# Expert layers: where the modulation's shift is added to the gathered tokens

## Chip, cores and metric

One core of a Trainium2 chip runs the whole program, in one launch. The metric is the device time of an execution in microseconds (us); the time before is the median of three runs.

## What is computed

Two blocks of two layers each work on 512 tokens of 1024 features. The change concerns the first block, whose two layers each end in a mixture of 16 experts. Every token goes to two experts, after a norm and a modulation: a scale and a shift per feature, the same for all tokens.

```python
h = modulate(rms_norm(x, norm_ffn_g[i]), sh2, sc2)      # h * (1 + scale) + shift
x = x + g2[:, None, :] * hier_moe(h, moe_wg[i], moe_bg[i], moe_we[i], moe_be[i],
                                  moe_w_gate[i], moe_w_up[i], moe_w_down[i])
...
for e in range(N_EXPERTS):
    a = jax.nn.silu(t @ w_gate[e]) * (t @ w_up[e])
    out = out + combine[:, e:e + 1] * (a @ w_down[e])
```

## The kernel before

The kernel is written in a tile framework: a scheduler puts the instructions of each engine in a fixed order when the program is built, and assigns the tiles of a pool to its buffers then. Each engine runs its own list in that order and waits on semaphores.

An expert layer (`moe`, layers 0 and 1) computes only the tokens that an expert was given. The norm's scaled tokens, without the shift, are written to DRAM (`h2d`). For each expert GpSimd (POOL) issues a `gather` (L969): an indirect DMA that brings the expert's 128 rows of tokens into a tile `xg`, 128 tokens by 1024 features, 512 KB. `moe_xt` then turns `xg` feature-major: eight transposes of 128x128 on TensorE (PE) in two halves `xT` (`moe_xt1`, L1120). In each half a matmul follows that multiplies `shT`, the shift as rows on 16 partitions, with `shs`, a selection of these rows, and so adds the shift to the transposed tokens in PSUM (L206, `xT<-shs,shT`). ScalarE (ACT) and VectorE (DVE) split the half into a high part `xh` (ACT, L221) and a low part `xl` (DVE, L222); float32 products are made of three matmuls of such parts (`mm3`).

Layer 0 has 17 blocks of this kind (16 experts and a spare block for an expert that holds over 128 tokens), layer 1 has 16: 33 in all. I call each a round. A round's weights come in six chunks of 512 KB: four of gate and up (`gu`), two of down (`dn`). SyncE (SP) loads them into a ring of buffers: five `raw` tiles, two `xt` tiles, and `NRING` tiles (7 before) of the pool "pair", which has 25 tiles of 128x1024 and also holds `xg`, `xh`, `xl` and the results `Y`. Each chunk is split by ACT (`wh<-pre`) and DVE (`wl<-pre,wh`) into one of four pairs of `wsplit` tiles, which PE frees as it goes. On PE a round is: the transposes of the next round's tokens, 12 `gu` matmuls, two transposes `aT` of the round before, 12 more `gu` matmuls, 12 `dn` matmuls of the round before. ACT also evacuates `Y<-dn` and takes the Silu (`sg`); POOL issues the store of each `Y` to DRAM (L1166).

Before the rounds of a layer the router's results are turned into lists of tokens (`route`, `slots`), and `overflow` places a branch that is taken only when an expert holds more than the blocks there are. All engines read a number (`eid`) that DVE wrote and pass that branch. `GA = 4` gathers are asked for ahead of the rounds.

Of the kernel before, what the change touches and what calls it, by code (L numbers as in the profile page):

```python
# [9 lines left out]
FT = mybir.dt.float32  # L10
# [31 lines left out]
class First:  # L42
    """The first products W^T x after a norm, from x as it is: the factor per token comes after the products. The first
    four tiles of columns are fed tile by tile of x, as they become final."""

    def __init__(self, k, W, cols, scale, shift=None):
        """shift: a shift after the norm and a bias of the products; what both add to the products is left in bias."""
        self.k, self.W, self.cols, self.scale, self.shift = k, W, cols, scale, shift
        self.in_moe = False
        self.R, self.P, self.w, self.bias, self.S, self.n = [], {}, [], None, None, 0  # L50

    def feed(self, k, h=None):
        """Tile k of x is final, or half h of its tokens."""
        K = self.k
        n, hs = (512, 0) if h is None else (256, h)
        per = 512 // n
        cs = slice(hs * n, hs * n + n)
        if k == 0:
            self.P[hs] = [K.acc("f") for _ in range(4 // per)]
        if k % 4 == 0 and not hs:  # L60
            for ci, c in enumerate(self.cols):
                self.w.append(K.wtiles(self.W, D, k, 4, c, use=lambda r, k0: self.shifted(r, k0, ci, 2),
                                       q=K.nc.gpsimd if k and WL & 1 and self.in_moe else None)[0][1])
        if not hs:
            self.R.append(K.p("xr"))
        a = self.R[k]
        ah, al = a[:, cs], a[:, 512 + cs.start:512 + cs.stop]
        K.split(K.x[k][:, cs], ah, al, self.scale(k))
        for i in range(4):
            o = k % 4 * 256 + i % 2 * 128  # L70
            wh, wl = (y[:, o:o + 128] for y in self.w[k // 4 * 2 + i // 2])
            K.mm3(self.tile(i, hs, n), wh, wl, ah, al, k == 0 and i % per == 0,
                  k == KD - 1 and i % per == per - 1)
        if k == KD - 1 and cs.stop == 512:
            self.biases(4)
            self.w = None

    def shifted(self, raw, k0, ci, n):
        """The shift times four tiles by 256 columns, a quarter of the partitions each."""
# [27 lines left out]
    def tiles(self, rB):  # L107
        """Yields the four products, scaled, in SBUF."""
# [9 lines left out]
    def more(self, cols, rB):  # L118
        """Yields four more."""
# [16 lines left out]
class Base:  # L136
# [29 lines left out]
    def filter_done(self):  # L166
        """The filter's banks go to the products and the rest."""
        self.fctx.close()
        self.xp = self.pool("extra", 2)
        self.banks(self.ctx, acc=AC, misc=8 - AC)  # L170
# [46 lines left out]
    def split(self, src, h, l, scale=None):  # L217
        """src (times a per-partition scale) = h + l, both of 12 significant bits."""
# [13 lines left out]
    def wload(self, dma, n=1024, alloc=None, use=None):  # L232
        """Load n columns per partition and split them."""
# [18 lines left out]
    def wtiles(self, W, K, k0, kt, c0, alloc=None, use=None, q=None):  # L252
        """Chunks of at most 4 k-tiles by 256 columns."""
# [8 lines left out]
    def fm(self, W, c0, ncols, acts, k0=0, kt=8, K=1024):  # L262
        """Feature-major products: yields (tile, PSUM) per 128 columns of W."""
# [13 lines left out]
    def fm2(self, W, c0, ncols, acts, k0=0, kt=8, K=1024, pools=()):  # L277
        """As fm, all columns with half the tokens before the other half: yields (tile, half, PSUM)."""
# [32 lines left out]
    def rstd_from(self, ss, n):  # L311
        """ss: the sums of squares of eight tiles, or tiles whose sum over tiles and partitions is it, per token."""
# [22 lines left out]
    def norm_sb(self, ss, n):  # L335
        """The factor per token: on partitions, and as a row on all partitions."""
# [7 lines left out]
    def norm_half(self, ss, n, h, r, R=None, more=()):  # L344
        """The same for half h of the tokens; the row stays in PSUM unless R is given."""
# [18 lines left out]
    def sq_acc(self, ss, src, h=None):  # L364
        """Square a tile, or half h of its tokens; four at a time are summed over the partitions."""
# [12 lines left out]
    def flow(self, tasks, window):  # L378
        """Tasks (generators) started in order, one a round, at most window of them at a time, a stage a round each."""
# [26 lines left out]
    def range_red(self, w, k):  # L406
        """w modulo 2 pi, in [-pi, pi]."""
# [30 lines left out]
class Mla:  # L438
# [7 lines left out]
    def ada_vec(self, i, nm):  # L446
        """A modulation vector of layer i: 256 of its values in each quarter of the partitions."""
# [58 lines left out]
    def x_in(self):  # L506
        """The input, feature-major, split, and the first norm's factor per token."""
# [53 lines left out]
    def rope_apply(self, out, y, nm, t, nh, u=None):  # L561
        """Rotate y (heads of 64) into both halves of out (heads of 2 x 64)."""
# [12 lines left out]
    def mla_pre(self, r1, H, out):  # L575
        """Latents, and the keys, values and queries of two heads."""
# [98 lines left out]
    def kv(self, g, c, out, done):  # L675
        """Keys and values of two heads, as tasks."""
# [42 lines left out]
    def queries(self, g, cT, out, done):  # L719
        """Queries of two heads, as tasks."""  # L720
# [49 lines left out]
    def attend(self, KP, o, K, V, Q, QP):  # L770
        """Two heads, as tasks of a head and 128 queries."""
# [53 lines left out]
    def resid(self, W, acts, i, g):  # L825
        """x += g * (W^T acts); the squares' sums for the next norm."""
# [26 lines left out]
NRING = 7  # L853
# [3 lines left out]
class Moe:  # L857
# [3 lines left out]
    def moe_consts(self):  # L861
# [12 lines left out]
        self.shT = [None, None]  # L874
        self.shs = self.const("shs", [16, 8], FR)
        nc.vector.tensor_add(self.shs, self.ident[:16, 0:8], self.ident[:16, 8:16])
# [12 lines left out]
    def router_prep(self, i):  # L889
        """Fold the modulation into the router: scaled weights, and the bias of the shift."""  # L890
# [8 lines left out]
    def router(self):  # L899
        """Router products with tokens on the partitions."""  # L900
# [8 lines left out]
    def moe_pre(self, i):  # L909
        """Before the products that end in x: the shift as a row, the first weights."""  # L910
        nc = self.nc
        sh = self.mod[i][:, ADA_OFF["sh2"]:ADA_OFF["sh2"] + 8]
        w = self.sm("sh", 16)
        self.split(sh, w[:, :8].bitcast(FR), w[:, 8:].bitcast(FR))
        P = self.ps("shT")
        nc.tensor.transpose(P[:16, :128], w, self.ident)
        self.shT[i] = self.const(f"shT{i}", [16, 128], FR)
        nc.scalar.activation(self.shT[i], P[:16, :128], AF.Copy)
# [7 lines left out]

    def moe_x(self, i, k):
        """As each tile of x is final: scale it, and multiply with the router."""
# [17 lines left out]
    def moe_load(self, i, ec, kind):  # L946
        """Load a chunk into a tile of one of three pools."""
# [5 lines left out]
    def chunk_dma(self, raw, i, e, c, q=None):  # L953
        """Two k-tiles of gate and up (c < 4), or a k-tile of down."""
# [4 lines left out]
    def moe(self, i, ss, first=None):  # L959
# [7 lines left out]
        def gather(e):  # L967
            xg[e] = self.p("xg", FT)
            nc.gpsimd.indirect_dma_start(out=xg[e], out_offset=None, in_=self.h2d[i],  # L969
                                         in_offset=bass.IndirectOffsetOnAxis(ap=idx[e], axis=0))  # L970

# [41 lines left out]
        for t in range(NT):  # L1013
# [10 lines left out]
            nc.scalar.dma_start(self.h2d[i][t * 128:(t + 1) * 128, :], ht)  # L1024
        self.slots(R, 0, 2, idx)
# [6 lines left out]
        for e in range(2, GA):  # L1032
            gather(e)
        XT[0] = self.moe_xt(xg.pop(0))
        prev = None
        for e in range(N):
# [4 lines left out]
            if e + GA < N and e + GA > 1:  # L1041
                gather(e + GA)
            at = []
# [16 lines left out]
        if N > 16:  # L1060
            w = [self.wload(lambda r, c=c: self.chunk_dma(r, i, self.edyn, 4 + c, nc.scalar)) for c in range(2)]
        C = self.combine_load(i, R)
# [8 lines left out]
    def moe_zero(self):  # L1071
        """The row of a product that comes in another way."""
# [44 lines left out]
    def moe_xt1(self, X, a, P):  # L1117
        """Half of a block's tokens' features, feature-major, with the shift."""
        for k in range(4):
            self.nc.tensor.matmul(P[:, k * 128:(k + 1) * 128], X[:, (a * 4 + k) * 128:(a * 4 + k + 1) * 128], self.ident,  # L1120
                                  is_transpose=True, start=k == 0, stop=False)
        self.mm(P, self.shT[self.li][:16, :], self.shs[:16, a * 4:a * 4 + 4][:, :, None].to_broadcast([16, 4, 128]),
                False, True)
# [144 lines left out]
    def pieces(self, src, dst):  # L1268
        """Three bfloat16 pieces whose sum is src."""
# [46 lines left out]
    def overflow(self, i, R, spare):  # L1316
        """Blocks of 128 tokens of the experts that hold more than 128, under a branch. With a spare block
        the first of them is among the experts, and always computed (its slots may all be empty)."""
# [69 lines left out]
        def block(j):  # L1388
# [4 lines left out]
                                         in_offset=bass.IndirectOffsetOnAxis(ap=q[16], axis=0))  # L1393
            for a, P in enumerate((P0, P1)):
# [33 lines left out]
        def finish(idx, late):  # L1428
            """The spare block's slots, and the row of each product of each token."""
# [34 lines left out]
    def combine(self, i, C, L, first):  # L1464
        """The sum of each token's products into x; with products to come, half the tokens before the other."""
# [62 lines left out]
class Hyena:  # L1528
# [13 lines left out]
    def filter_gen(self, z, w, tn, nd):  # L1542
# [21 lines left out]
        def taps(o, c2, i):  # L1564
            """Filter responses of a channel tile, split into even and odd taps, position-major."""
# [189 lines left out]
    def table(self, src, split, whole):  # L1755
        """A table and its two parts."""
# [88 lines left out]
class Mix:  # L1845
# [13 lines left out]
    def first(self, kind, l):  # L1859
        """The first products after a norm in layer l."""  # L1860
# [9 lines left out]
    def tail(self, z, zs, prod, evac, g, nxt):  # L1870
        """The last columns of z, x += rmsnorm(z) * g and the next norm's factor, half the tokens after the other."""
# [38 lines left out]
    def conv(self, y, src, taps, bias=None):  # L1910
        """Causal: y[t] = sum_d taps[d] src[t-d], the first tap on ScalarE."""
# [269 lines left out]
def blocks(W):  # L2181
    """[K, N] as contiguous blocks of 256 columns by up to 4 x 128 rows, a row of the block per partition."""
# [9 lines left out]
def layout(I):  # L2192
    """The inputs as the kernel loads them: moved, padded with zeros and repeated, never computed with."""
# [125 lines left out]
```

## Time and profile before

| | |
|---|---|
| three runs | 2946.20, 2946.41, 2952.02 us; median 2946.41 |
| profiled execution | its span, first to last instruction, 2939.1 us; what lies around the span is 7.3 us against the median |
| PE busy | 2806.4 us (95%) |
| DVE busy | 1914.6 us (65%) |
| ACT busy | 1300.5 us (44%) |
| POOL busy | 144.8 us (5%) |
| rounds' transposes, layer 0 | first at 448.7 us, last at 614.8 us of the span |
| rounds' transposes, layer 1 | first at 1011.95 us, last at 1166.3 us of the span |

No separate time is given for the profiled execution, so its own time is taken as the span, and the median of the runs as the time to which differences are added. "Busy" counts the time in which an engine has at least one instruction under way. Averages over the whole span hide the stage at hand: in the rounds DVE is far busier than 65%.

### The profile page before, as it was taken

The page shows a single profiled execution, that of the slowest core. Times are in us where ns is not written, and L with a number is a line of the kernel's source. Part 1 is how long each engine was busy: PE and PEld are TensorE (multiplying, and loading weights), DVE is VectorE, ACT ScalarE, POOL GpSimd, SP SyncE. Part 2 cuts the span into 40 slices and gives each one's busy share as a digit, 9 for nine tenths or more (in the row PEclk, how much of TensorE's full clock was granted, in tenths as well). Part 3 has the DMA queues.
Part 4 walks back from the last instruction along what each step waited for, and adds up shares of the span by engine and source line. Part 5 has one row for each costly group of instructions (what it writes and reads, how often), then busy time and mean ns, then how long its engine had stood idle before and what let it go on. Part 6 is the DMA issues. An engine that isn't in the chain of part 4 may idle for free.

```text
span 2939.1 us, 38010 instructions
## 1 busy us (share of the span) xinstructions
PE 2806.4 (95%) x14430; PEld 2223.5 (76%) x14430; DVE 1914.6 (65%) x3260; ACT 1300.5 (44%) x2222; POOL 144.8 (5%) x191
## 2 busy tenths in 40 slices
PE   6899988999999799899999999999999999999998
PEld 2666766767866577678887888888878888888887
DVE  5776748986776498579935486264679645484363
ACT  4566746874312488443224354243343224353341
POOL 0111001110000111200000000000000000000000
PEclk8999998999999899999999999999999999999999
DMA  6666368962443498422222223223222332132321
GB/s 209 220 216 218 113 232 283 388 257 76 160 157 127 146 356 338 151 94 79 100 92 89 83 74 108 93 90 97 80 83 83 101 100 86 58 103 93 106 90 47
DMA packets 128148, 416.96 MB, mean 142 GB/s; under 512 B 13888, under 2 KB 24336, under 8 KB 127952
## 3 DMA queue, kind: packets, MB, share of 16 engines
q1 hardware_dynamic: 96128, 335.06, 32.9%
q0 software_dynamic: 12304, 44.58, 4.1%
q10 hardware_dynamic: 19520, 34.76, 3.4%
q8 instruction: 117, 1.92, 0.3%
q14 instruction: 79, 0.65, 0.1%
HBM read 380.78 MB, written 33.56 MB: 141 GB/s over the span
## 4 chain that ended last, share of the span: by engine, by line
PE 61%; DVE 2%; POOL 1%; issue 1%; DMA 0%; ACT 0%; POOLq 0%; DVEq 0%
PE acc L206 46%; PE gu L206 3%; PE f L206 3%; PE v L206 2%; PE dn L206 1%; PE ss L206 1%; PE nh L206 1%; PE xT L1120 1%; PE o L206 1%; DVE pre L1855 0%; PE S L206 0%; PE xT L206 0%; DVE uy L1918 0%; DMA y<-ys,pos 0%; PE bc L206 0%
## 5 line engine op out<-in xcount | busy, mean ns | idle before, releaser
L206 PE MATMUL acc<-X,wh 128*128 128x512 f32 x2432 | 755.8, 391 | 0.8 <-ACT X L221 0.7
L222 DVE TENSOR_TENSOR wl<-raw,wh 128x1024 fp32r<-128x1024 f32 (+1 forms) x338 | 411.2, 1220 | 408.2 <-ACT wh L221 396.6
L221 ACT ACTIVATE wh<-raw 128x1024 fp32r<-128x1024 f32 (+2 forms) x362 | 370.2, 1027 | 449.5 <-PE acc L206 376.0
L206 PEld LDWEIGHTS acc<-X,wh 128*128 128x128 f32 x2432 | 454.8, 188 | 97.6 <-issue 2.2
L206 PE MATMUL acc<-X,wl 128*128 128x512 f32 x1216 | 473.9, 390 | 0.0
L206 PEld LDWEIGHTS acc<-X,wl 128*128 128x128 f32 x1216 | 228.4, 188 | 47.1
L222 DVE TENSOR_TENSOR wl<-pre,wh 128x1024 fp32r<-128x1024 f32 x184 | 222.0, 1223 | 31.0 <-ACT wh L221 27.2
L206 PE MATMUL acc<-f,wh 128*128 128x512 f32 (+1 forms) x912 | 228.7, 349 | 0.0
L221 ACT ACTIVATE wh<-pre 128x1024 fp32r<-128x1024 f32 x184 | 191.4, 1058 | 37.3 <-PE gu L206 33.2
L206 PEld LDWEIGHTS acc<-f,wh 128*128 128x128 f32 x912 | 157.0, 189 | 25.2 <-issue 3.3
L2086 DVE SCALAR_TENSOR_TENSOR cfa<-sb,par,cfa 128x511 f32<-128x511 f32 (+15 forms) x240 | 163.2, 733 | 1.8 <-ACT cfa L2081 1.8
L206 PE MATMUL acc<-xr,wh 128*128 128x512 f32 x448 | 138.9, 391 | 0.0
L206 PE MATMUL acc<-f,wl 128*128 128x512 f32 (+1 forms) x384 | 136.4, 355 | 0.0
L1918 DVE SCALAR_TENSOR_TENSOR uy<-acc,par,uy 128x511 f32<-128x511 f32 (+1 forms) x128 | 95.7, 748 | 58.5 <-ACT uy L1914 56.3
L206 PE MATMUL f<-xr,wh 128*128 128x256 f32 x640 | 126.7, 291 | 1.8 <-ACT xr L224 1.8
L206 PE MATMUL gu<-wh,xh 128*128 128x512 f32 x264 | 112.1, 425 | 1.9 <-ACT wh L221 1.9
L206 PEld LDWEIGHTS f<-xr,wh 128*128 128x128 f32 x640 | 102.1, 192 | 13.5 <-issue 9.1
L206 PE MATMUL gu<-wl,xh 128*128 128x512 f32 x264 | 106.3, 403 | 0.9 <-DVE wl L222 0.8
L206 PE MATMUL gu<-wh,xl 128*128 128x512 f32 x264 | 106.6, 404 | 0.0
L206 PEld LDWEIGHTS acc<-xr,wh 128*128 128x128 f32 x448 | 83.9, 188 | 18.4 <-issue 1.2
L206 PE MATMUL f<-xr,wl 128*128 128x256 f32 x320 | 91.1, 286 | 0.0
L206 PE MATMUL acc<-xr,wl 128*128 128x512 f32 x224 | 87.6, 391 | 2.4 <-DVE wl L222 2.4
(511 smaller groups left out, 5153.9 us busy)
## 6 DMA issues: line engine op xcount, KB each, us to landing
pre<-in_moe SPq DMA_DIRECT2D x184, 512.0 KB, 8.1
raw<-in_w_in SPq DMA_DIRECT2D x106, 512.0 KB, 3.3
raw<-in_ada_w SPq DMA_DIRECT2D x96, 512.0 KB, 5.0
raw<-in_w_up SPq DMA_DIRECT2D x88, 512.0 KB, 3.3
raw<-in_w_down SPq DMA_DIRECT2D x40, 512.0 KB, 3.4
ys<-Y POOLq DMA_DIRECT2D x28, 512.0 KB, 7.1
raw<-in_hy_w_in SPq DMA_DIRECT2D x22, 512.0 KB, 3.6
kd<-K ACTq DMA_DIRECT2D x32, 256.0 KB, 2.5
```

The costliest lines, as they stand in the source:

```text
L206: return self.nc.tensor.matmul(o, a, b, start=st, stop=sp)
L221: nc.scalar.activation(h, src, AF.Copy)
L222: nc.vector.tensor_sub(l, src, h.bitcast(FT))
L1120: self.nc.tensor.matmul(P[:, k * 128:(k + 1) * 128], X[:, (a * 4 + k) * 128:(a * 4 + k + 1) * 128], self.ident, is_transpose=True, start=k ...
L1918: nc.vector.scalar_tensor_tensor(y[:, d:], src[:, :512 - d], taps[d], y[:, d:], op0=OP.mult, op1=OP.add)
L2086: v.scalar_tensor_tensor(c[j][:, d:], glu[i][:, :512 - d], self.pc(f"cf_conv_w{l}", (30 - d) * 4 + i), c[j][:, d:], op0=OP.mult, op1=OP.add)
```

## The change

The tokens get their shift in SBUF, right after they were gathered, and the matmul into the transposes goes. `shift_row` spreads the shift as one row over all 128 partitions (`shB`, a tile of the pool "pair", made by eight matmuls of 128x128 and two copies by ACT). `shift(e)` adds it to `xg[e]`: one TENSOR_TENSOR of 128x1024 in float32, on DVE for the first round of a layer, on POOL for all others. `NRING` goes from 7 to 6. `shT`, `shs` and their preparation in `moe_pre` go. Docstrings were taken out as well, which moves line numbers: the gather keeps L969, the add is L973, the transposes become L215, the store of `Y` L1171.

```diff
-NRING = 7
+NRING = 6
...
     def moe_pre(self, i):
-        nc = self.nc
-        sh = self.mod[i][:, ADA_OFF["sh2"]:ADA_OFF["sh2"] + 8]
-        w = self.sm("sh", 16)
-        self.split(sh, w[:, :8].bitcast(FR), w[:, 8:].bitcast(FR))
-        P = self.ps("shT")
-        nc.tensor.transpose(P[:16, :128], w, self.ident)
-        self.shT[i] = self.const(f"shT{i}", [16, 128], FR)
-        nc.scalar.activation(self.shT[i], P[:16, :128], AF.Copy)
...
+    def shift_row(self, i):
+        self.shB = self.p("shB", FT)
+        for a in range(2):
+            P = self.ps("shB")
+            for k in range(4):
+                self.mm(P[:, k * 128:(k + 1) * 128], self.m_(i, "sh2", a * 4 + k).to_broadcast([128, 128]), self.ident,
+                        True, True)
+            self.nc.scalar.activation(self.shB[:, a * 512:(a + 1) * 512], P, AF.Copy)
...
+        def shift(e, eng=nc.gpsimd):
+            eng.tensor_tensor(xg[e], xg[e], self.shB, op=OP.add)
...
+        self.shift_row(i)
         self.slots(R, 0, 2, idx)
...
         for e in range(2, GA):
             gather(e)
+        for e in range(GA - 1):
+            shift(e, nc.gpsimd if e else nc.vector)
         XT[0] = self.moe_xt(xg.pop(0))
...
             if e + GA < N and e + GA > 1:
                 gather(e + GA)
+            if e + GA <= N:
+                shift(e + GA - 1)
...
+        self.shB = None
         C = self.combine_load(i, R)
...
     def moe_xt1(self, X, a, P):
-        for k in range(4):
-            self.nc.tensor.matmul(P[:, k * 128:(k + 1) * 128], X[:, (a * 4 + k) * 128:(a * 4 + k + 1) * 128], self.ident,
-                                  is_transpose=True, start=k == 0, stop=False)
-        self.mm(P, self.shT[self.li][:16, :], self.shs[:16, a * 4:a * 4 + 4][:, :, None].to_broadcast([16, 4, 128]),
-                False, True)
+        self.tr4(P, [X[:, (a * 4 + k) * 128:(a * 4 + k + 1) * 128] for k in range(4)])
```

Two places show how the instructions move.

POOL in the middle of layer 0, before: `xg` tiles are gathered, `Y` tiles are stored, and nothing waits for a gather on this engine.

```order
L969 DMA xg1304_6289<-h2d0_360,ix1243_6070 128x1024
L1166 DMA ys0_362<-Y1301_6271 128x1024
L969 DMA xg1334_6397<-h2d0_360,ix1243_6070 128x1024
L1166 DMA ys0_362<-Y1331_6379 128x1024
L969 DMA xg1377_6648<-h2d0_360,ix1370_6539 128x1024
L1166 DMA ys0_362<-Y1361_6487 128x1024
```

The same place in the change:

```order
L969 DMA xg1274_6173<-h2d0_358,ix1243_6063 128x1024
L1171 DMA ys0_360<-Y1271_6155 128x1024
L973 TENSOR_TENSOR xg1274_6173<-xg1274_6173,shB1095_4893 128x1024
L969 DMA xg1304_6280<-h2d0_358,ix1243_6063 128x1024
L1171 DMA ys0_360<-Y1301_6262 128x1024
L973 TENSOR_TENSOR xg1304_6280<-xg1304_6280,shB1095_4893 128x1024
```

Each add stands behind the gather of the very tile that it works on, and ahead of the next gather, so POOL waits there for the transfer to land.

DVE ahead of the branch of layer 0, before: the lists of rounds 2 and 3 (`oh`) are partly made ahead of the branch (`eid` is the number that it reads, `ovx` the places of the combine).

```order
L1282 TENSOR_TENSOR oh1136_5652<-iotab_341,rb1082_4839 128x512
L1272 CAST rw1084_4845<-M1079_4816 128x64
L1330 CAST eid1105_4943<-ovf1104_4938 128x1
L1434 SCALAR_TENSOR_TENSOR ovx1106_4959<-iotas_337,M1079_4816 128x64
L1437 TENSOR_TENSOR ovx1106_4959<-M1079_4816,ovx1106_4959 128x64
L1438 TENSOR_REDUCE ovx1106_4959<-ovx1106_4959 128x4
L1331 TENSOR_LOAD eid1105_4943
L1421 COMPARE_AND_BRANCH
```

And in the change:

```order
L1444 TENSOR_REDUCE ovx1107_4963<-ovx1107_4963 128x4
L1445 TENSOR_SCALAR ovx1107_4963<-ovx1107_4963 128x8
L1446 SCALAR_TENSOR_TENSOR ovx1107_4963<-ovx1107_4963 128x8
L973 TENSOR_TENSOR xg1103_4923<-xg1103_4923,shB1095_4893 128x1024
L1336 TENSOR_LOAD eid1106_4947
L1427 COMPARE_AND_BRANCH
```

The first round's add stands ahead of the branch on DVE and waits for that round's gather; the four `oh` that stood there stand behind the branch now.

## Rows read from the trace of the kernel before

**Rows 1.** Windows: busy us and count of each engine, clock, DMA share, GB/s
```profile
core 0: us, PE busy (x) PEld busy (x) DVE busy (x) ACT busy (x) POOL busy (x), PEclk, DMA share, GB/s
560.00:600.00 40.00, 40.00 (x184) 30.82 (x183) 35.91 (x41) 33.68 (x47) 4.23 (x6) 1.00 1.03 418
1120.00:1160.00 40.00, 40.00 (x185) 30.94 (x185) 35.98 (x39) 33.41 (x47) 3.20 (x5) 1.00 1.03 419
```

**Rows 2.** Timeline of PE, one round: start us, duration us, engine, line, op
```profile
573.38 0.50 PE L206 MATMUL gu<-wh,xh 128*128 128x512 f32 x1
...
576.40 0.48 PE L206 MATMUL gu<-wh,xh 128*128 128x512 f32 x1
...
582.49 0.48 PE L206 MATMUL xT<-shs,shT 16*128 16x512 f32 x1
582.90 0.66 PE L1120 MATMUL xT<-par,xg 128*128 128x128 f32 x4
583.49 0.48 PE L206 MATMUL xT<-shs,shT 16*128 16x512 f32 x1
583.89 0.50 PE L206 MATMUL gu<-wh,xh 128*128 128x512 f32 x1
```

**Rows 3.** Timelines of ACT and DVE in the same round
```profile
573.98 2.00 ACT L221 ACTIVATE wh<-pre 128x1024 fp32r<-128x1024 f32 x2
...
575.07 3.50 DVE L222 TENSOR_TENSOR wl<-pre,wh 128x1024 fp32r<-128x1024 f32 x3 [0.26 <-ACT wh L221]
```

**Rows 4.** Groups by shape on DVE: count, busy us, mean ns, idle before
```profile
L222 DVE TENSOR_TENSOR wl<-pre,wh 128x1024 fp32r<-128x1024 f32 x184 | 222.0, 1223 | 31.0 <-ACT wh L221 27.2 <-DMA pre<-in_moe 0.4
L222 DVE TENSOR_TENSOR xl<-xT,xh 128x512 fp32r<-128x512 f32 x66 | 43.1, 684 | 5.0 <-ACT xh L221 4.4
...
L222 DVE TENSOR_TENSOR aT<-aT,aT 128x256 fp32r<-128x256 f32 x33 | 13.8, 417 | 1.0 <-ACT aT L221 1.0
L1138 DVE TENSOR_TENSOR sg<-sg,gu 128x256 f32<-128x256 f32 x33 | 13.7, 415 | 1.7 <-ACT sg L1137 1.7
```

**Rows 5.** Groups by shape on POOL: the fills by a ramp
```profile
L864 POOL IOTA iotas<- 128x512 f32 x1 | 0.6, 556 | 0.4 <-POOLq L2306 0.4
...
L867 POOL IOTA pidx<- 128x1 f32 x1 | 0.1, 134 | 0.0
```

**Rows 6.** Timelines of POOL and DVE: POOL's small two-input instructions, and DVE beside one
```profile
104.07 0.69 POOL L308 TENSOR_TENSOR rk<-vk,mhalf 128x2 f32<-128x2 f32 x1 [2.14 <-DVE vk L306]
...
153.85 1.01 POOL L308 TENSOR_TENSOR rq<-vq,mhalf 128x4 f32<-128x4 f32 x1 [4.64 <-DVE vq L304]
...
1318.28 1.52 DVE L2086 SCALAR_TENSOR_TENSOR cfa<-sb,par,cfa 128x510 f32<-128x510 f32 x2
1318.43 1.44 POOL L308 TENSOR_TENSOR r<-v,mhalf 128x4 f32<-128x4 f32 x1 [73.23 <-DVE v L306]
...
1333.35 0.74 DVE L2086 SCALAR_TENSOR_TENSOR cfa<-sb,par,cfa 128x508 f32<-128x508 f32 x1
```

**Rows 7.** POOL's gathers: one in the timeline, their landing, waits for weight chunks
```profile
542.93 0.97 POOL L969 DMA_INDIRECT xg<-h2d,ix  x1 [0.30 <-issue]
...
DMA to landing us min/median/max: 4.1/8.4/11.0
...
  DMA pre<-in_moe: 0.7, 3
```

**Rows 8.** Timelines of POOL, DVE and PE at the start of layer 0's rounds, and that gather's landing
```profile
439.18 1.09 POOL L969 DMA_INDIRECT xg<-h2d,ix  x1 [6.29 <-DVE route L1256]
...
444.58 0.22 DVE L1438 TENSOR_REDUCE ovx<-ovx 128x4 f32<-128x64 f32 x1
...
448.56 0.69 DVE L1282 TENSOR_TENSOR oh<-iotab,rb 128x512 bf16<-128x512 bf16 x1 [3.76 <-DVEq L1421]
...
xg<-h2d,ix POOLq DMA_INDIRECT x1, 4.3
```

More of the change, by code (lines that the diff above doesn't have):

```diff
@@ L873, in moe_consts @@
         nc.vector.memset(self.onesb, 1.0)
-        self.shT = [None, None]
-        self.shs = self.const("shs", [16, 8], FR)
-        nc.vector.tensor_add(self.shs, self.ident[:16, 0:8], self.ident[:16, 8:16])
+        self.shB = None
         self.key = self.const("key", [128, 16])
@@ L1061, in moe @@
             w = [self.wload(lambda r, c=c: self.chunk_dma(r, i, self.edyn, 4 + c, nc.scalar)) for c in range(2)]
+        self.shB = None
         C = self.combine_load(i, R)
@@ L1393, in block @@
                                          in_offset=bass.IndirectOffsetOnAxis(ap=q[16], axis=0))
+            v.tensor_add(X, X, self.shB)
             for a, P in enumerate((P0, P1)):
```

## The prediction

> **What bounds the kernel now.** I read the windows first, to see which engine is full in the rounds; then PE's timeline of one round, for the period and the price of the matmul that goes; then ACT and DVE in that round, for who hands PE its operands; then POOL, which gets the new work.
>
> In both expert layers PE is busy for 40.00 of 40 us, DVE for 35.91 and 35.98, ACT for 33.68 and 33.41, and the DMA engines stand at 1.03 of their time with 418 GB/s, while POOL is busy for 4 us [rows 1]. So three resources are near their ends at once. A round lasts 583.89 - 573.38 = 10.51 us on PE [rows 2]. DVE works 35.91/40 of it, 9.44 us, and has 1.07 us to spare. A round moves eight tiles of 512 KB (six chunks, one gather, one store), 4.19 MB; at 418 GB/s that takes 10.03 us, 0.48 us less than the round.
>
> The operands come just in time. The first of DVE's three splits that start at 575.07 lasts about 1.23 us and ends near 576.30; the matmul that uses this chunk starts at 576.40 [rows 2, 3]. A tenth of a microsecond of delay on DVE is a delay of PE. Weights themselves are not late: ACT waited for a chunk's transfer three times, 0.7 us together [rows 7].
>
> **The sum, against the profiled execution.** Its span is 2939.1 us; the median of the runs, 2946.4 us, has 7.3 us more around it, which the change leaves alone. I add differences to 2946.4.
>
> *Removed: two matmuls of the shift per round.* From the start of one to the start of the next instruction it is 0.41 us (582.49 to 582.90) and 0.40 us (583.49 to 583.89) [rows 2], 0.81 us per round; 33 rounds have 66 of them. PE alone would then need 9.70 us. The transfers need 10.03, so a round in which nothing else is late gains 0.48 us, and 0.81 us at the most while chunks that are in the ring already last.
>
> *Added: an add of 128x1024 on POOL for all but the first round of a layer, 31 in all.* No row has a POOL instruction of this size. From below: DVE does this shape in 1.22 us [rows 4]. From above, by POOL's own rows: the ramp of 512 elements takes 556 ns and that of one element 134 ns [rows 5], 0.83 ns per element written; two-input instructions take 1.01 us for four elements and 0.69 us for two [rows 6], which leaves 0.37 us without elements; two streams read and one written, each at 0.83 ns and none beside another, are 3 x 0.85 + 0.37 = 2.9 us. I take 2.1 us: two reading streams (1.70) and 0.37, with the writing beside them, because POOL's own rows are nearer to the case than DVE's.
>
> POOL has the time for it. The question is what DVE does meanwhile. A POOL instruction with four elements that began 0.15 us into a DVE instruction with two SBUF inputs took 1.44 us instead of 1.01 [rows 6]: it waited until DVE's was over (0.74 us long, to about 1319.02). The reverse is not shown well: the second DVE instruction ended at 1319.80, before POOL's did at 1319.87, so the small POOL instruction did not keep DVE out until its end. But it reads four elements, where the add reads two streams of 1024 for most of its time. So DVE's loss is somewhere between zero and the whole 2.9 us.
>
> The Trainium skill, in "SBUF — State Buffer", section "Who interferes with whom", says that a DVE instruction with two SBUF inputs and a GpSimd instruction that reads SBUF share one read interface, and that the later one is shut out for the whole of the earlier one. The trace agrees for POOL's wait (1.44 against 1.01 us) and not for the end of the small one (1319.80 against 1319.87). The skill's "GPSIMD Engine Reference", section 3.1, has 4497 ns for an add of 2048 elements; half of it, an estimate, is 2.25 us; put in the place of 2.1 us below, it gives 0.6 us per round and a sum near 2955.
>
> I take it that DVE is held while POOL reads, in its weight splits (`wl<-pre,wh`, both inputs in SBUF), and not in `xl`, `aT` and `sg`, which read PSUM. These last 2 x 0.68 + 0.42 + 0.42 = 2.20 us per round [rows 4], and 1.07 us is idle: 3.27 of 10.51 us, 31%. The loss is 2.1 x 0.69 = 1.45 us per add. By DVE's sum a round takes 9.44 + 1.45 = 10.89 us, 0.38 more than before. If each hold reaches PE whole, since the slack is 0.1 us, it is 1.45 - 0.81 = 0.64 more. I take 0.5 us.
>
> *Where the adds fall.* Those of rounds 1 to 5 run in the start of a layer, where DVE has room. The adds of rounds 6 to 16 and 6 to 15, 21 in all, fall between full rounds: 21 x 0.5 = +10.5 us. About six rounds at the layers' ends have no add beside them: 6 x -0.48 = -2.9 us.
>
> *The start of a layer.* DVE reached the branch at 444.58 + 0.22 = 444.80 and was through it at 448.56, 3.76 us later [rows 8]. The first gather lands at 439.18 + 4.3 = 443.5, so the add on DVE waits little for it, but lasts 1.22 us ahead of the branch, where four `oh` of some 0.6 us and the places of the combine change sides. I put DVE some 0.8 us later at the branch, and with the lists behind it the first `gu` 1.0 us later. Rounds 1 and 2 lose four of the removed matmuls there, 4 x 0.4 = 1.6 us, while PE is what ends last. Together -0.6 us per layer, -1.2 us.
>
> *At nothing.* The eight small matmuls and two copies that make `shB` stand between `rank` and the first list on PE, where PE waits for DVE anyway; if they don't fit, the first gather is later by at most a microsecond per layer. The ring's seventh tile: 13 chunks remain and no chunk is late today [rows 7]; if that cover goes, every later chunk costs its transfer's delay. The preparation of `shT` saves some tenths.
>
> Sum: +10.5 - 2.9 - 1.2 = +6.4 us, 2952.8, so **2953 us**. What runs of this kernel can tell from no change is about 0.2%, 5.9 us; the forecast stands on that edge.
>
> **Rivals.**
>
> *POOL's reading does not hold DVE.* Then only the removed matmul counts. For it speaks the second DVE instruction that ended before POOL's [rows 6]; against it, POOL's own wait there, which shows a common way in. 27 rounds (all but the first three of each layer) gain 0.48 us where transfers bind: -13.0 - 1.2 gives 2932 us; with 0.81 us it would be 2923. It decides as soon as the loss per add is under 1.07 us, DVE's spare time. Chance 0.28.
>
> *POOL's queue becomes the bound.* In the new order each add waits for its own gather to land, with the next gather and the next store behind it. A turn is the landing (8.4 us in the middle, 11.0 at most, [rows 7]), the add of 2.1 and an issue of about 0.6: 11.1 us, at most 13.7, against 10.51 per round. The lead covers this: round 13's gather was issued at 542.93 and its transposes run at 582.49 [rows 2, 7], 39 us later, and ten turns lose 6 to 32 us. Once a turn passes 10.5 + 3.9 = 14.4 us the lead is used up. If landings grow to 13 us because the stores of `Y` and the buffers come late, a turn is 15.7, and ten lose 52, 13 more than the lead: 26 us for two layers, about 2975 with the smaller gain of the rest. Chance 0.13.
>
> *The two cancel.* A loss near 1.0 us per add leaves the rounds as they are: 2946 us. Chance 0.09.
>
> **How the numbers follow.** The forecast's case has 0.50, and its own range goes from an add of 1.6 us to one of 2.7 us, 2942 to 2964; of this 0.30 is slower by over 0.2%, 0.18 within it, 0.02 faster. With the rivals: slower 0.30 + 0.13 = 0.43, within 0.18 + 0.09 = 0.27, faster 0.02 + 0.28 = 0.30. The range reaches from the first rival's 2932 to the second's 2975, taken as 2976; what lies outside is a gain of 0.81 us in all rounds, or a ring that runs empty.
>
> **What would show it.** Right: adds on POOL of 2 to 3 us, `wl<-pre` on DVE whose mean rises from 1223 ns by a quarter of a microsecond (1.45 us over six splits), waits of PE's `gu` for DVE, and a period of 10.9 to 11.1 us. For the first rival: `wl` still at 1223 ns, a period near 10.0, DMA share still 1.03. For the second: `xT` on PE waiting for POOL's add. I am wrong altogether if the start of a layer moves by more than 3 us, or if chunks come late.

## The result, and the profile after

The changed kernel takes **2981.84 us** (median of 4 runs, 2981.09 to 2987.82) against 2948.78 us (4 runs) of the kernel before on the same chip: 33.1 us more, a ratio of 1.0113 with a 95% interval of 1.0101 to 1.0125. The forecast was 2953 with a range of 2932 to 2976. The sign is right, the size is not, and the result lies outside the range.

The windows of the changed kernel, with the columns of [rows 1]:

```profile
560.00:600.00 40.00, 35.39 (x162) 27.72 (x162) 39.04 (x37) 30.50 (x43) 18.01 (x12) 0.99 0.98 366
1120.00:1160.00 40.00, 36.52 (x190) 28.49 (x189) 39.62 (x50) 30.33 (x42) 18.96 (x9) 1.00 0.92 347
```

PE is no longer full: 35.39 and 36.52 of 40 us, where it had 40.00 [rows 1]. DVE has become full: 39.04 and 39.62 against 35.91 and 35.98. The DMA engines moved less (366 and 347 GB/s), so transfers don't set the pace. DVE counts *fewer* instructions in the first window (37 against 41) and is busy longer. The groups by shape on DVE and POOL say which of them grew, beside [rows 4]:

```profile
L222 DVE TENSOR_TENSOR wl<-pre,wh 128x1024 fp32r<-128x1024 f32 x184 | 257.4, 1434 | 10.2 <-ACT wh L221 9.3
L222 DVE TENSOR_TENSOR xl<-xT,xh 128x512 fp32r<-128x512 f32 x66 | 42.5, 681 | 11.6 <-ACT xh L221 7.7 <-ACT wh L221 3.4 <-issue 0.4
L222 DVE TENSOR_TENSOR aT<-aT,aT 128x256 fp32r<-128x256 f32 x33 | 13.7, 415 | 0.2 <-ACT aT L221 0.2
...
L973 POOL TENSOR_TENSOR xg<-xg,shB 128x1024 f32<-128x1024 f32 x31 | 87.2, 2813 | 128.0 <-DMA xg<-h2d,ix 126.3 <-DVE ovx L1279 1.6
```

The weight splits `wl<-pre,wh`, both inputs in SBUF, went from 1223 to 1434 ns, 35 us of busy time in all. `xl` (681 ns, was 684) and `aT` (415, was 417), which read PSUM, did not change. One add in the timelines of POOL and DVE, in a full round:

```profile
582.64 2.39 POOL L973 TENSOR_TENSOR xg<-xg,shB 128x1024 f32<-128x1024 f32 x1 [7.64 <-DMA xg<-h2d,ix]
```
```profile
581.03 1.21 DVE L222 TENSOR_TENSOR wl<-pre,wh 128x1024 fp32r<-128x1024 f32 x1
582.16 0.42 DVE L222 TENSOR_TENSOR aT<-aT,aT 128x256 fp32r<-128x256 f32 x1
582.90 4.36 DVE L222 TENSOR_TENSOR wl<-pre,wh 128x1024 fp32r<-128x1024 f32 x2 [0.32 <-ACT wh L221]
587.18 0.41 DVE L1143 TENSOR_TENSOR sg<-sg,gu 128x256 f32<-128x256 f32 x1
```

Two splits, 2.35 us where nothing disturbs them (as in the run with fills, below), take 4.36. They end at 587.26, 2.23 us behind the add's end at 585.03, as if DVE had begun only then. PE sees it at once, in its timeline of that round:

```profile
584.09 0.61 PE L206 MATMUL dn<-wh,aT 128*128 128x512 f32 x2
586.17 0.50 PE L206 MATMUL dn<-wl,aT 128*128 128x512 f32 x1 [1.47 <-DVE wl L222]
```

`xl`, from PSUM, keeps its time beside an add that runs until 1155.10 (POOL's row 1150.88 below), and the split behind it, at 1153.95, is held:

```profile
1152.75 1.28 DVE L222 TENSOR_TENSOR xl<-xT,xh 128x512 fp32r<-128x512 f32 x2
1153.95 2.23 DVE L222 TENSOR_TENSOR wl<-pre,wh 128x1024 fp32r<-128x1024 f32 x1
```

The start of a layer has a second loss. The timelines of ACT, PE and DVE there, the counterpart of [rows 8]:

```profile
440.16 0.60 ACT L925 ACTIVATE shB<-shB 128x512 f32<-128x512 f32 x1 [3.05 <-PE shB L206]
440.22 0.33 ACTq L1027 DMA_DIRECT2D h2d<-ht  x1
441.76 0.60 ACT L925 ACTIVATE shB<-shB 128x512 f32<-128x512 f32 x1 [1.01 <-PE shB L206]
```
```profile
438.07 3.66 PE L206 MATMUL shB<-par,mod 128*128 128x128 f32 x16
```
```profile
442.14 0.16 DVE L1309 TENSOR_TENSOR ix<-ixf 128x2 int32<-128x2 f32 x1
```

The store of the last tokens stands behind a copy of the row on ACT's queue, and that copy waits for the row's matmuls. The first gather needs that store and its list of tokens (`ix`), and both come late. The store starts 8.88 us behind the router's factor (440.22, POOL's `r` at 431.34), 5.80 us before. The list is written 10.80 us behind the factor (442.14), 9.80 us before, since the row's matmuls hold PE for 3.66 us ahead of the list's own. The gather is issued at 443.74, 12.40 us behind the factor. Before it was 10.25 us (439.18 - 428.93).

### The profile page after: what moved, and what is told of

Read it like the earlier page. It is cut to its first block, busy times and chain, and to the rows that moved or that the text cites. A ratio compares the mean times of both kernels' runs of the same rounds, so it can differ in the third digit from the quotient of the medians.

```text
span 2979.3 us, 37910 instructions
## 1 busy us (share of the span) xinstructions
PE 2796.1 (94%) x14394; PEld 2221.9 (75%) x14394; DVE 1962.3 (66%) x3259; ACT 1297.0 (44%) x2222; POOL 244.7 (8%) x222
## 4 chain that ended last, share of the span: by engine, by line
PE 55%; DVE 2%; issue 1%; POOL 1%; DMA 0%; ACT 0%; POOLq 0%; DVEq 0%; ACTq 0%
PE acc L206 46%; PE f L206 3%; PE v L206 1%; PE ss L206 1%; PE nh L206 1%; PE o L206 1%; DVE pre L1861 0%; PE S L206 0%; DVE wl L222 0%; DVE uy L1924 0%; PE gu L206 0%; PE bc L206 0%; DMA y<-ys,pos 0%; DVE X L222 0%; POOL r L308 0%
## 5 line engine op out<-in xcount | busy, mean ns | idle before, releaser
L222 DVE TENSOR_TENSOR wl<-raw,wh 128x1024 fp32r<-128x1024 f32 (+1 forms) x338 | 411.2, 1220 | 407.8 <-ACT wh L221 396.2
L222 DVE TENSOR_TENSOR wl<-pre,wh 128x1024 fp32r<-128x1024 f32 x184 | 257.4, 1434 | 10.2 <-ACT wh L221 9.3
L221 ACT ACTIVATE wh<-pre 128x1024 fp32r<-128x1024 f32 x184 | 188.4, 1061 | 17.4 <-PE gu L206 9.7
L308 POOL TENSOR_TENSOR r<-v,mhalf 128x4 f32<-128x4 f32 x13 | 16.5, 1270 | 1087.9 <-DVE v L306 1087.9
L308 POOL TENSOR_TENSOR rh<-vh,mhalf 128x2 f32<-128x2 f32 x18 | 13.1, 728 | 1120.3 <-DVE vh L306 1120.3
L973 POOL TENSOR_TENSOR xg<-xg,shB 128x1024 f32<-128x1024 f32 x31 | 87.2, 2813 | 128.0 <-DMA xg<-h2d,ix 126.3
```

The lines of the kernel that those rows point to most:

```text
L221: nc.scalar.activation(h, src, AF.Copy)
L222: nc.vector.tensor_sub(l, src, h.bitcast(FT))
L308: nc.gpsimd.tensor_tensor(r, v, self.mhalf[:, :n], op=OP.pow)
L973: eng.tensor_tensor(xg[e], xg[e], self.shB, op=OP.add)
```

## The experiments

Three theories. **A**: each add holds DVE's splits and lists (the forecast's mechanism, mis-sized). **B**: POOL's in-order queue, in which an add waits for its own gather with stores and gathers behind it. **C**: the start of a layer costs most of it. All times are medians of 4 to 10 executions, taken beside the kernel before; that was 2951.64 us with the first four runs, 2949.85 with the next four and 2951.55 with the last two. These medians and the 2948.78 of the result differ by up to 2.9 us, so smaller differences between runs decide nothing.

**Without the adds.** `shift` does nothing; the rest is the change.

```
-            eng.tensor_tensor(xg[e], xg[e], self.shB, op=OP.add)
+            pass
```

> Leaves out the shift of the gathered tokens (the row shB is still made and held, the order of the start of a layer stays the changed one); only the adds are gone, 31 on POOL and 2 on DVE. Theory A (the adds hold DVE's weight splits, PE waits for wl): wl back to 1223 ns, rounds of 10.0 to 10.5 us, 2935 to 2950. Theory B (POOL's queue: each add waits for its own gather's landing, gathers and stores of Y come late): the same time, since the waits go too, so this run gives the price of all adds and not their way. Theory C (the start of a layer and the moved lists cost most of it): above 2960, with the first gu 3 to 6 us later than before in each layer.

Measured 2926.1 us, ratio 0.9911 (0.9894 to 0.9929). So the adds cost 56 us (2981.8 - 2926.1), and what is left of the change gains 25 us, more than any theory allowed. PE's timeline shows where from, and the windows stand under it:

```profile
574.37 1.03 PE L215 MATMUL xT<-par,xg 128*128 128x128 f32 x8
575.15 0.48 PE L206 MATMUL gu<-wh,xh 128*128 128x512 f32 x1
...
583.67 1.03 PE L215 MATMUL xT<-par,xg 128*128 128x128 f32 x8
```
```profile
560.00:600.00 40.00, 40.00 (x197) 33.24 (x196) 38.39 (x44) 35.83 (x52) 3.22 (x5) 1.00 1.03 411
1120.00:1160.00 40.00, 40.00 (x193) 33.09 (x193) 38.67 (x45) 36.51 (x52) 4.00 (x7) 1.00 1.03 411
```

The period is 583.67 - 574.37 = 9.30 us, 1.2 less than the 10.51 of [rows 2]. The matmuls of the shift were 0.81 of that. Most of the rest is that all eight transposes run as one piece now: 575.15 - 574.37 = 0.78 us from the first of them to `gu`. In the kernel before it was 583.89 - 581.96 = 1.93 us: 0.81 for the two matmuls, and 0.53 and 0.59 for the four transposes ahead of each, 0.34 more than now:

```profile
581.96 0.60 PE L1120 MATMUL xT<-par,xg 128*128 128x128 f32 x4
```

The windows show the other half of the story: without any add, DVE is already busy for 38.39 of 40 us, 0.37 us from full in a 9.3 us round. And transfers don't bind: at 411 GB/s a round of 9.3 us brings 3.8 of the 4.19 MB that it uses, and what was loaded ahead covers the difference for the length of a layer (in the first window ACT split 25 chunks while SP asked for 22 and POOL for one gather). The waits for a chunk's transfer were one of 0.3 us in all; before there were three, 0.7 us.

**One input instead of two.**

```
-            eng.tensor_tensor(xg[e], xg[e], self.shB, op=OP.add)
+            eng.tensor_copy(xg[e], xg[e])
```

> Leaves out the shift: POOL's 128x1024 instruction stays at its place, waits for the same gather, reads and writes xg, but has one input instead of two. Theory A, in the form that two readers of SBUF share one way in: a one-input instruction of POOL still reads, so if any read holds DVE then wl stays at 1.35 us or more and the time within 10 us of 2982; if only a second input does, wl is back at 1.22 to 1.26 us and the time 2940 to 2955. Theory B (POOL's queue): wl may be back, but the time stays above 2970, as the waits for gathers are the same.

Measured 2935.72 us, 0.9945 (0.9926 to 0.9964). POOL's and DVE's timelines, one copy in a round:

```profile
564.88 1.53 POOL L973 COPY xg<-xg 128x1024 f32<-128x1024 f32 x1 [4.10 <-DMA xg<-h2d,ix]
```
```profile
564.28 3.20 DVE L222 TENSOR_TENSOR wl<-pre,wh 128x1024 fp32r<-128x1024 f32 x2 [0.32 <-ACT wh L221]
```

The copy holds DVE too: two splits take 3.20 us, not 2.36. But alone it lasts 1.04 us (its shortest of 31) where the add's shortest is 2.33, so it can hold for less; `wl` has a mean of 1277 ns. My expectation knew only "any read holds" with 1.35 us or "a second input holds" with 1.22 to 1.26; it had forgotten that half the reading takes half the time. Theory B is out as the main cause: the copies, too, wait for their gathers for 110 us in all, and the run is 46 us faster than the change.

**The same place, nothing read.** Two fills in the place of each add.

```
-            eng.tensor_tensor(xg[e], xg[e], self.shB, op=OP.add)
+            for n in range(2):
+                eng.memset(xg[e], 0.5)
```

> Leaves out the shift and the tokens: two fills of 128x1024 on POOL stand in the place of each add, wait for the same gather and write the same tile, but read nothing (the blocks' tokens are a constant). If POOL holds DVE by reading: wl at 1.22 to 1.24 us and 2924 to 2938, as without adds, the waits for gathers notwithstanding. If POOL's writing holds DVE too, or if POOL's queue costs: wl above 1.3 us, or wl at 1.22 and 2945 or more.

Measured 2935.55 us, 0.9951 (0.9935 to 0.9968). One pair of fills on POOL, and DVE beside it:

```profile
563.00 1.97 POOL L974 MEMSET xg<- 128x1024 f32 x2 [7.08 <-DMA xg<-h2d,ix]
```
```profile
560.56 3.50 DVE L222 TENSOR_TENSOR wl<-pre,wh 128x1024 fp32r<-128x1024 f32 x3
563.97 0.41 DVE L1144 TENSOR_TENSOR sg<-sg,gu 128x256 f32<-128x256 f32 x1
564.30 2.35 DVE L222 TENSOR_TENSOR wl<-pre,wh 128x1024 fp32r<-128x1024 f32 x2
```

POOL is busy for 1.97 us of writing and the splits keep their 1.22 us (mean of 184: 1220 ns). It is POOL's reading that holds DVE. This run has the waits of theory B, 158 us of them against 126 in the change, and no hold: so B by itself is worth some 9.5 us (2935.55 - 2926.1).

**The adds one block later on POOL.**

```
-        for e in range(GA - 1):
+        for e in range(GA - 2):
...
-            if e + GA <= N:
-                shift(e + GA - 1)
+            if e + GA - 2 < N:
+                shift(e + GA - 2)
```

> Computes the reference. Each add stands one round later on POOL (the block two rounds ahead instead of three, two adds at the start instead of three), so its gather has long landed and POOL should not wait for it. Theory A (DVE held by the adds): the wait of 126 us on POOL goes, the time falls by 0 to 8 us, to 2974 to 2982; wl stays at 1.40 to 1.45 us. Theory B (POOL's queue): gathers come back to one per round without delay, the time falls by 15 to 25 us, to 2957 to 2967.

Measured 2979.53 us, 1.0110 (1.0084 to 1.0135). This number falls where A put it, but the run decides nothing: the add still waits for its gather, for 118.5 us against 126.3. In the rounds the scheduler put each add back behind its own gather and the next store, where it had been. Theory B had to be told apart by the copy and the fills.

**All adds on DVE.**

```
-            eng.tensor_tensor(xg[e], xg[e], self.shB, op=OP.add)
+            nc.vector.tensor_tensor(xg[e], xg[e], self.shB, op=OP.add)
```

> Computes the reference: all 33 adds on DVE, POOL has none. If a POOL add costs DVE as much as its own time beside it (1.9 to 2.3 us, by the held rows of the changed kernel), then the add done by DVE itself, 1.22 us, is cheaper: DVE's round of 9.0 us becomes 10.2 to 10.3, and the time is that of the run without adds, 2926, plus 33 times 1.0 to 1.2: 2959 to 2966, below the change's 2982. If DVE's capacity is not what binds (the loss is in POOL's queue or in the start of the layer), 2926 to 2940. If the hold costs less than an add on DVE, above 2982.

Measured 2958.84 us, 1.0027 (1.0014 to 1.0039), 23 us below the change. DVE's groups:

```profile
L222 DVE TENSOR_TENSOR wl<-pre,wh 128x1024 fp32r<-128x1024 f32 x184 | 218.2, 1219 | 13.7 <-ACT wh L221 9.7 <-issue 3.5
L973 DVE TENSOR_TENSOR xg<-xg,shB 128x1024 f32<-128x1024 f32 x33 | 40.3, 1220 | 11.0 <-DMA xg<-h2d,ix 10.9
```

DVE does the add in 1.22 us and 33 of them cost 32.7 us (2958.84 - 2926.1), 1.0 each. POOL, meant to relieve DVE, costs it more than the work itself.

**The row made earlier.** `self.shift_row(i)` moves from behind the tokens' stores into `moe_pre`.

```
     def moe_pre(self, i):
+        self.shift_row(i)
...
-        self.shift_row(i)
         self.slots(R, 0, 2, idx)
```

> Computes the reference: the row on all partitions is made before the products that end in x (where the transposed shift was prepared before the change) and no more between rank and the first list; all adds stay. If making the row there is what makes the first gu late (from the router's factor to the first gu 28 us against 24.7 before): first gu 2 to 3.5 us earlier in each layer, 2974 to 2979. If the adds hold DVE's lists and this is the whole loss of the start: 2979 to 2984, and the third block's transposes as late as in the change (54 us behind the router's factor in the first layer).

Measured 2976.16 us, 1.0091 (1.0074 to 1.0108), 5.7 us below the change. The first gather is back at 10.26 us behind the router's factor (441.26 - 431.00), so making the row at that place, on PE and in ACT's queue, costs some 3 us a layer. The transposes of block 3 (counted from 0) still come 50.0 us behind the factor, against 45.6 before and 54.5 in the change, so the adds have a part in the start as well. The next two runs measure it.

**The adds of the rounds alone, and of the start alone.** The one has `if e >= GA:` ahead of the add (25 adds left), the other `if e < GA:` (8 left).

> Leaves out the shift of the first four blocks of each layer (two adds on DVE, six on POOL, all in the start of a layer); the 25 others stay on POOL. By the times of the transposes, change against the run without adds, the start costs 12.9 us in the first layer and 4.7 in the second, the rounds 18.5 and 22.4. If these parts are independent: 2982 - 18 = 2964 (2958 to 2970). If the rounds are late only because the start left the lists and the ring late: 2930 to 2945. If the start's loss would be made up in the rounds anyway: 2974 to 2982.

> Leaves out the shift of all blocks but the first four of each layer. If start and rounds are independent: 2926 + 18 = 2944 (2938 to 2950). If the rounds are late only because of the start: 2965 or more. If the start's loss is made up in the rounds: 2926 to 2934.

Measured 2971.50 us, 1.0078 (1.0059 to 1.0098), and 2934.08, 0.9942 (0.9924 to 0.9961). The 25 adds in the rounds cost 45.4 us (2971.5 - 2926.1), 1.8 each; the 8 in the start 8.0 us (2934.1 - 2926.1), or 10.3 by the other difference (2981.8 - 2971.5). The parts add up but for some 2 us, and C is out as the main cause. I had put the start at 18 us by the times of the transposes in one execution each, and some of what is lost there is made up later.

**The kernel before with the smaller ring.**

```
-NRING = 7
+NRING = 6
```

> The kernel before with a ring of six tiles instead of seven, nothing else: the price of the tile that the row takes. Priced at nothing in the forecast: within 5 us of before (2944 to 2956). If the ring's lead matters: 2955 or more, with waits for weight chunks above 5 us.

Measured 2945.86 us, 0.9985 (0.9975 to 0.9994): the seventh tile was worth nothing.

**The shift in the tokens before they are stored.** The row is made in `moe_pre`; DVE, not ACT, moves the tokens out of PSUM and adds it in the same instruction. No add in the rounds, no matmul, seven tiles in the ring.

```
-                if a and t >= HA:
-                    nc.vector.tensor_scalar(ht[:, sl], P, r[:, t:t + 1], None, op0=OP.mult)
-                else:
-                    nc.scalar.activation(ht[:, sl], P, AF.Copy, scale=r[:, t:t + 1])
+                nc.vector.scalar_tensor_tensor(ht[:, sl], P, r[:, t:t + 1], self.shB[:, sl], op0=OP.mult, op1=OP.add)
```

> Computes the reference in another way: the row is made where the small transposed shift was prepared before the change, and DVE adds it to the tokens as it moves them out of PSUM, before they are stored for the gathers; no add in the rounds, no matmul of the shift, ring of seven tiles. Theory A and B: rounds of 10.0 to 10.5 us, as in the run without adds; the start of a layer loses 1 to 4 us to eight two-input instructions on DVE of some 0.75 us beside the router's chain; 2930 to 2948. Theory C (the moved order at the start costs most): 2950 or more, if DVE's part at the start is as late as in the changed kernel.

Measured **2926.88 us**, 0.9916 (0.9900 to 0.9933): faster than both kernels, by 25 us than the one before and by 55 us than the change. The rounds in PE's timeline:

```profile
576.00 1.03 PE L215 MATMUL xT<-par,xg 128*128 128x128 f32 x8
576.79 0.48 PE L206 MATMUL gu<-wh,xh 128*128 128x512 f32 x1
...
585.31 1.03 PE L215 MATMUL xT<-par,xg 128*128 128x128 f32 x8
```

9.31 us a round, as without adds. A block's tokens are gathered from rows that every block shares, so the shift belongs to the 512 tokens once, not to each of the 33 blocks.

## Why the prediction was wrong

Point by point, each forecast term against its run:

| term | forecast, us | measured, us | from |
|---|---|---|---|
| matmuls removed, 33 rounds | -16 | -31 | 2926.1 - 2951.6, less 5.7 for the row |
| adds in the rounds | +21 | +45 | rounds' adds alone - no adds |
| adds in the start | +2 | +8 to +10 | start's adds alone; change - rounds' adds alone |
| making the row | 0 | +6 | change - row early |
| ring of six | 0 | 0 | ring of six - before |
| sum | +6.4 | +28 to +30 | whole change: +33.1 |

(In the forecast's -16 stand 27 rounds at 0.48 us and 3.2 us in the starts; in its +21, 21 adds that turn -0.48 into +0.5.) Some 3 to 5 us of the 33.1 belong to no row of the table; the medians of the kernel before alone differ by nearly that much (2948.8 to 2951.6).

**What held.** The mechanism was right: POOL's reading shuts out DVE's two-input instructions and leaves those with a PSUM input alone. The signs that I had named for it came nearly true: `wl` longer by 0.21 us, PE waiting for DVE, a full round of 11.2 us where I had put 10.9 to 11.1. I put the add at 2.1 us; its shortest is 2.33. The estimate from the price in the Trainium skill ("GPSIMD Engine Reference", section 3.1), 2.25 us, was nearer to 2.33 than mine. The skill's rule in "SBUF — State Buffer", section "Who interferes with whom", agrees with the runs on both sides: two-input instructions of DVE are shut out by a reader on POOL (3.20 us for two splits beside the copy), and not by an instruction that only writes (1220 ns beside the fills).

**The step that failed** is the conversion of this hold into time: "If each hold reaches PE whole, since the slack is 0.1 us, it is 1.45 - 0.81 = 0.64 more. I take 0.5 us", on top of "DVE works 35.91/40 of it, 9.44 us, and has 1.07 us to spare". I took DVE's spare time from the round *with* the matmuls. Once they are gone, PE can run a round in 9.30 us and DVE's work fills it but for 0.37 us. The forecast counted 0.98 us an add (from -0.48 to +0.5); the runs with 25 adds and with none show 1.8.

The hold itself was too small as well. These windows span the same three full rounds (9 to 11 of layer 0, three adds in the change) in the kernel before, in the run without adds and in the change:

```profile
552.40:583.90 31.50, 31.50 (x146) 24.31 (x145) 29.04 (x33) 27.67 (x39) 5.53 (x6) 1.00 1.02 411
```
```profile
547.10:575.20 28.10, 28.10 (x140) 23.24 (x138) 26.59 (x31) 26.12 (x37) 5.53 (x6) 1.00 1.03 411
```
```profile
566.90:600.50 33.60, 28.99 (x138) 22.66 (x137) 32.64 (x31) 26.42 (x37) 16.06 (x9) 1.00 0.98 378
```

DVE is busy for 32.64 us instead of 26.59, 2.0 us an add where I had 1.45, and a round takes 1.8 us more (33.60 against 28.10). So a hold costs about its length, less the little that DVE has to spare. Averaged over the 25 adds of the rounds, `wl` and the lists' `oh` are 35 us longer than without adds (33.4 and 1.8), 1.41 us an add: close to my 1.45, but by luck, since this mean takes in adds beside which the splits lost little or nothing.

"Since the slack is 0.1 us" was a misreading of [rows 2, 3]. Counted through in the order in which PE uses the chunks, six `gu` matmuls each, the split that ends near 576.30 isn't the one that the matmul at 576.40 uses: it is the fourth of its round, and PE comes to it at 578.10, 1.8 us later. In rounds 10 to 15 of layer 0 the splits of `gu` were 1.8 to 4.1 us ahead of PE. A hold reaches PE because DVE's work of a round no longer fits into the round, not because each split is just in time.

**Where the miss came out.** Against the kernel before, the three rounds above went from 31.50 to 33.60 us, 0.7 a round, and I had forecast 0.5: the gain of the removal and the cost of an add were both put at about half, and in full rounds the two errors nearly cancel, which is luck. By the starts of `gu` in PE's timelines, one execution of each kernel, the miss stands at both ends of the layers, where the terms for the start ("-0.6 us per layer") and for the rounds without an add ("6 x -0.48 = -2.9 us") failed outright:

| stretch, both layers together | forecast, us | change - before, us |
|---|---|---|
| router's factor to round 2 | -1.2 | +10.3 |
| to round 12 in layer 0, 11 in layer 1 (16 adds) | +8.0 | +7.4 |
| to the last round (5 adds, and the rounds without any) | -0.4 | +12.9 |

My own sign of being wrong altogether, a start of a layer that moves by more than 3 us, came true in layer 0: its first `gu` is 28.2 us behind the router's factor, 24.7 before (27.6 and 24.9 in layer 1).

At the layers' ends theory B has its part. Rows of POOL, ACT and PE in round 11 of layer 1, which took 18.1 us:

```profile
1150.88 4.22 POOL L973 TENSOR_TENSOR xg<-xg,shB 128x1024 f32<-128x1024 f32 x1 [6.96 <-DMA xg<-h2d,ix]
...
1157.03 0.59 POOL L1171 DMA_DIRECT2D ys<-Y  x1
```
```profile
1166.66 1.09 ACT L1170 ACTIVATE Y<-dn 128x512 f32<-128x512 f32 x2 [6.69 <-DMA ys<-Y]
```
```profile
1169.72 0.79 PE L206 MATMUL gu<-wh,xh 128*128 128x512 f32 x1 [5.44 <-ACT wh L221]
```

ACT had finished a `Y` at 1151.67, but its store stands on POOL behind an add that waited 6.96 us for its gather. ACT then waits 6.69 us for a store of `Y` to land, with a weight chunk's split behind that wait, and PE 5.44 us for the split. The runs bear this out: against the run without adds, the last stretch of the table is 10.8 us longer with the fills, which have the queue and no hold, and 3.1 us longer with all adds on DVE; in the change it is 17.4 us longer.

Such waits of PE have a second price. PE's timeline at the first layer's start, where lists held by adds made a split of `xT` late:

```profile
478.07 0.69 PE L215 MATMUL aT<-par,sg 128*128 128x128 f32 x2 [7.35 <-DVE xl L222]
...
478.99 0.63 PE L206 MATMUL gu<-wl,xh 128*128 128x512 f32 x1
...
482.67 0.39 PE L206 MATMUL gu<-wl,xh 128*128 128x512 f32 x1
```

After a wait of 7.35 us the matmuls take 0.63 us each, and then 0.39; the granted clock was 0.50 from 478 to 482 (the lower of its two levels, 1.2 GHz) and 1.00 from 483 to 487. Over all rounds, from the first stretch at full clock on, it was 0.95 and 0.96 in the two layers of the change, 1.00 and 1.00 in the kernel before, 0.99 and 1.00 without the adds:

```profile
462.10:644.40 182.30, 159.72 (x765) 125.19 (x763) 171.55 (x216) 130.94 (x183) 68.37 (x42) 0.95 0.87 315
1045.80:1210.00 164.20, 145.72 (x704) 115.72 (x703) 153.91 (x163) 122.76 (x172) 69.03 (x41) 0.96 0.89 325
```

By these shares the change's rounds hold some 30 us at the lower level; at half speed PE loses at most 15 us there, an estimate. No run separates the clock's part from that of the waits.

**The other terms.** The removal was mis-sized for two reasons: the price of 0.41 us per matmul left out what the break between the two groups of transposes cost, and the limit by transfers of 10.03 us a round left out the lead of the ring, which covers a layer. "DVE has room" in the start of a layer was wrong: its lists are a chain of short instructions, and a short one that meets an add waits for all of it, as these rows of POOL and DVE show:

```profile
470.10 2.84 POOL L973 TENSOR_TENSOR xg<-xg,shB 128x1024 f32<-128x1024 f32 x1
```
```profile
470.50 0.21 DVE L1357 TENSOR_TENSOR ovx<-M,ovx 128x64 f32<-128x64 f32 x1
470.63 2.34 DVE L1277 CAST rhn<-ovx 128x4 bf16<-128x4 f32 x1
472.88 0.21 DVE L1358 TENSOR_REDUCE ovx<-ovx 128x4 f32<-128x64 f32 x1
```

The add itself first gives way to the two-input instruction at 470.50 (it lasts 2.84 us, its shortest is 2.33), and then the cast is held until the add is over.

The row's matmuls, costed at nothing because PE waits there anyway, did not find room: they take 3.66 us, and the first list came 1.0 us later. I also missed ACT's queue, where a copy of the row came to stand ahead of a store that the first gather waits for.

**The rivals.** That the hold doesn't reach DVE is refuted by `wl`. That POOL's queue becomes the bound gave 2975, close to the measured time, but mostly for a reason that isn't so: POOL's waits are there, and late stores of `Y` stop the last rounds, as that rival had it, but by themselves they cost some 9.5 us.

## What to carry to other kernels

When a change shortens the engine that is the bound, measure the cover of everything else against the *new* period: DVE had 1.07 us to spare in a round of 10.51, and 0.37 in the round of 9.30 that the change itself made possible. An idle engine that shares a way to memory with a full one is no free place: an add that DVE does in 1.22 us cost 1.0 us there and 1.8 on POOL in the rounds. And before finding an engine for work per block, look for the place where it is done once per token.

## What the hardware showed that I had not expected

- A one-input cast of four elements to bf16 on DVE took 2.34 us beside an add on POOL (row 470.63 above), though it has no second input; a reduction that began 0.19 us into another add took 0.16 us, and the two-input instruction behind it 2.29, as the rows of POOL and DVE under this point show. The Trainium skill, in "SBUF — State Buffer", section "Who interferes with whom", names casts and copies among DVE's instructions that can take the second way in, and reductions as those that never do; here the trace agrees. The run with the row made earlier shows the same pair: a reduction of 0.21 us at 470.05 and a cast of 2.18 us at 470.18, beside an add that ends at 472.32.

```profile
465.42 2.53 POOL L973 TENSOR_TENSOR xg<-xg,shB 128x1024 f32<-128x1024 f32 x1 [1.19 <-DMA xg<-h2d,ix]
```
```profile
465.61 0.16 DVE L1348 TENSOR_REDUCE eidf<-ovf 128x1 f32<-128x16 f32 x1
465.69 2.29 DVE L1351 TENSOR_TENSOR ovf<-ovf 128x16 f32<-128x16 f32 x1
```

- The hold works both ways: here the engine whose instructions followed each other without a gap kept the other out. POOL's longest add, with DVE beside it:

```profile
1135.98 5.96 POOL L973 TENSOR_TENSOR xg<-xg,shB 128x1024 f32<-128x1024 f32 x1 [7.87 <-DMA xg<-h2d,ix]
```
```profile
1133.91 5.76 DVE L222 TENSOR_TENSOR wl<-pre,wh 128x1024 fp32r<-128x1024 f32 x5
1139.59 0.42 DVE L1143 TENSOR_TENSOR sg<-sg,gu 128x256 f32<-128x256 f32 x1
1139.92 3.10 DVE L222 TENSOR_TENSOR wl<-pre,wh 128x1024 fp32r<-128x1024 f32 x1
```

  Five splits in a row ran at full speed (5.76 us) while the add waited; an instruction that reads PSUM let POOL in, and the next split was held.
- Taking out the two matmuls with 16 rows, one behind each group of four transposes, gave back 1.2 us a round, of which their own time was 0.81.
